# Which engine subtracts the rests of the split mixer weights: VectorE and GpSimd, or VectorE alone

## Chip, cores and metric

The kernel runs on one core of a Trainium2 chip. The metric is the time of one execution on the device in microseconds; the times given are those of several runs of the same kernel, and the profile is of one more execution.

## What is computed

Two layers of an encoder on 256 tokens of 1024 features, all in float32. Each layer is a mixer and a mixture of experts, each followed by a layernorm on 1.414 times the residual plus the result:

```python
def _hybrid_mixer(h, w_in, lb, norm_g, w_out):
    proj = jnp.einsum('bsd,dc->bsc', h, w_in)
    hq, hf_f, hf_b, hi, hg, aq, ak, av = jnp.split(proj, cuts, axis=-1)
    y_hg = _hgrn2_group(hq, hf_f, hf_b, hi, hg, lb, norm_g)
    y_att = _dilated_attention_group(aq, ak, av)
    y = jnp.concatenate([y_hg, y_att], axis=-1).astype(h.dtype)
    return jnp.einsum('bsc,cd->bsd', y, w_out)

for l in range(DEPTH):
    mix = _hybrid_mixer(h, w_in[l], lb_all[l], hg_norm_g[l], w_out[l])
    h = _layernorm(DEEPNORM_ALPHA * h + mix, ln1_g[l], ln1_b[l])
    ffn = _hier_moe(h, router_w1[l], ..., ex_w_down[l])
    h = _layernorm(DEEPNORM_ALPHA * h + ffn, ln2_g[l], ln2_b[l])
```

The eight projections of `w_in` are 512 columns each: four recurrent heads (query, two forget gates, input, output gate) and eight attention heads (query, key, value). The experts are 32, two to a token, with weights of 6.3 MB each.

## The kernel before

**Split products.** The mixer's products run on TensorE (PE in the profile) in float32r, which is faster than float32 and less exact. So each operand is split into a head, its value rounded to float32r, and a rest, what the head leaves, and a product is three: head by head, head by rest, rest by head. For the weights this happens in `split_unit` (lines 284 to 308), as the weights arrive: ScalarE (ACT) copies a quarter of a unit to float32r, the head, and a second engine subtracts the head from the weight, the rest:

```python
hd, rest_ = S.copy(wh[:, i], raw[:, i]), eng(q).tensor_sub(wl[:, i], raw[:, i], wh[:, i])
```

That is line 302. A unit is [128, 2048], a quarter [128, 512]. A projection of `w_in` has two units, so 8 quarters, and there are 8 projections in a layer; `w_out` has 4 units, 16 quarters. The first quarter of all is split in two halves. In both layers this makes 161 heads and 161 rests.

**Which engine has the rest.** `eng` is given by the caller. `chunks` (lines 310 to 316) gives VectorE (V, DVE in the profile) for the projections in `V_UNITS`, the heads' input `U_HI` and the first forget gate `U_HF`, and GpSimd (G, POOL) for the other six and, in layer 1, for `U_HI` too. `out_unit` (line 645) gives VectorE the odd quarters of `w_out` and GpSimd the even ones. GpSimd has 120 of the 161 rests, VectorE 41.

**Buffers and order.** Raw weights lie in a ring of three units, head and rest in `NB` = 4 buffers of half a slot, a quarter to each; a buffer is free once PE's products of that quarter are done, and the load of a unit waits for the split of the unit three before it. The code is written in the order in which the work depends on each other, and a scheduler makes from it one fixed list of instructions for each engine, which the engine runs in order; `tc.high_priority()` around line 302 lets a head and its rest go ahead of what else could stand there. Loads are issued from SP's list, also in order.

**The mixer in time.** The projections come in the order input `U_HI`, forget gates `U_HF` and `U_HB`, query `U_HQ`, output gate `U_HG`, then attention's `U_AQ`, `U_AK` and `U_AV`. Their products have line 321 (356 for `U_HI` in layer 1). Beside them VectorE has the recurrent heads: the gates with their cumulative sums (lines 435 to 451), the exponents of the bottom blocks (512 to 521), and five levels of block lengths 8 to 128, each with a product with the query (532), four updates of the exponents (552 to 555) and masked copies (504); PE makes the levels' scores (497, 547). L556 on GpSimd adds two score matrices. Then come the heads' outputs (576 to 590), rotary embedding (400 to 405) and splitting (413) of attention's queries and keys, the scores (613), the softmax (618 to 627), transposes (667, 668), the products with the values (673), and the output projection (642). The first layernorm, the router and the experts follow; layer 1 begins with the second layernorm's transposed and split result, and its `U_HI` weights are split while that layernorm runs.

**Experts.** For each expert 12 loads of 0.5 MB go into half slots, in a fixed rotation over 45 of them, most of which the mixer uses before; a load waits until its half slot has been read.

The functions that the change touches:

Of the kernel before, what the change touches and what calls it, by code (L numbers as in the profile page):

```python
# [20 lines left out]
P = 128  # L21
# [4 lines left out]
CAP = 32  # L26
NL = 40            # columns of the router: 4 groups, 4 of padding, 32 experts
UNIT = 2048
HALF = UNIT // 2   # what a load of expert weights fills
NSLOT = 22         # slots of 8 KB, which half a slot more follows  # L30
NB = 4             # buffers of the split weights
NR = 3             # ring of the mixer's weights
S_H = 3            # recurrent heads, 7 slots
S_Q, S_SP = 10, 11
S_KV = S_H         # keys and values, after the recurrent heads' levels
S_P2 = S_H + 1     # half of the probabilities
S_X = 15           # x transposed, in layer 0
S_XS = 16          # x split, 2 slots
S_Y = 18           # mixer's outputs split, 2 slots, half a slot to 256 of the features
S_W = 20           # split weights, half a slot to a buffer  # L40
S_T = S_H + 2      # half a slot: sums transposed
S_N = S_Q          # second layernorm's factors
# [6 lines left out]
# the order in which the loads of the experts fill what the mixer leaves behind  # L49
# [4 lines left out]
# the last round leaves alone what the next layer begins with  # L54
# [11 lines left out]
V_UNITS = (U_HI, U_HF)  # L66
# [32 lines left out]
def trunk_kernel(ctx, tc, xT, x, w_in, w_out, ex, wr, br, lbl, ng, lng, lnb, lnt, cst, msk, lmk, out,  # L99
# [20 lines left out]
    def btiles():  # L120
        """[P, 1024], a bank to each half"""
        return [psb.tile([P, 512], F32, tag="b", name=nm("b")) for _ in range(2)]

    def fresh(slot, half, dtype=F32):
        """half a slot, once its last content has been read"""
        return per.tile([P, HALF], dtype, tag=f"s{slot}_{half}", name=nm(f"s{slot}_{half}"), bufs=1)

# [12 lines left out]
    # inputs, in the order in which they are needed  # L140
# [20 lines left out]
    # sigmoid's and hidden's buffers and transposed gates; before, the router's  # L161
# [18 lines left out]
    # lb of layer 1 = softmax over the two layers, second entry  # L180
# [8 lines left out]
    class Queue:  # L189
        """an engine whose instructions keep the order of the program"""  # L190
# [9 lines left out]
    def busy(n, rhs, o=None, weights=ident):  # L200
        """products that nothing reads: an array that waits, or that works on a few columns, has its clock halved"""
        o = o or wtile()
        for _ in range(n):
            PEq.matmul(o[:, 0:rhs.shape[-1]], weights, rhs, start=True, stop=True)
# [10 lines left out]
    def deviation(c):  # L215
        """mean and 1 / deviation of the rows of chunk c"""
        Vq.bn_aggr(ln_mv[c], ln_st[c])
        Sq.activation(ln_rs[c], ln_mv[c][:, 1:2], AF.Ln, bias=epsl)
        return Sq.activation(ln_rs[c], ln_rs[c], AF.Exp, scale=-0.5)

    def shift(c):
        """-mean / deviation"""
        Vq.scalar_tensor_tensor(ln_nb[c], ln_mv[c][:, 0:1], -1.0, ln_rs[c], op0=ALU.mult, op1=ALU.mult)
# [7 lines left out]
    def normal(c, f, src, g_, b_, dst):  # L231
        """all of it without the vector engine"""
        Sq.activation(dst, src, AF.Identity, scale=ln_rs[c], bias=ln_nb[c])
        Gq.tensor_mul(dst, dst, g_[:, fs[f]])
        Gq.tensor_add(dst, dst, b_[:, fs[f]])
# [4 lines left out]
    class Areas(dict):  # L240
        """half slots of the recurrent heads"""
# [8 lines left out]
    def head_and_rest(slot):  # L250
        """h transposed, split into a float32r head and an exact float32r rest, by halves of the features"""
# [8 lines left out]
    behind = {}  # what the first heads of a layer's weights are queued behind  # L260
    for l in range(depth):
        # ------------------------------------------------------------ mixer
# [5 lines left out]
        def y_split(k, n=1):  # L268
            """head and rest of the mixer's outputs k to k + n - 1"""
# [14 lines left out]
        def split_unit(w, eng, own=None, aft=(None,) * 4, chain=False):  # L284
            """the quarters of a unit, each as head and rest, in the rotating buffers or in slots of their own"""
            for q in range(4):
# [11 lines left out]
                # the first one of all in halves  # L298
                z = (slice(0, 256), slice(256, 512)) if l == 0 and q == 0 and w is first[0] else (slice(0, 512),)
                with tc.high_priority(), after(aft[q]), after(behind.get("wh")), after(behind.get("wl")):  # L300
                    for i in z:
                        hd, rest_ = S.copy(wh[:, i], raw[:, i]), eng(q).tensor_sub(wl[:, i], raw[:, i], wh[:, i])  # L302
# [7 lines left out]
        def chunks(u, i, own=None):  # L310
            """the quarters over k of a unit of w_in, split: [P, 2, 256] head and rest"""
# [3 lines left out]
            for q, wh, wl in split_unit(w, lambda q: G if first_ or u not in V_UNITS else V, own, aft, first_):  # L315
# [7 lines left out]
        def proj_ch(u):  # L323
            """for each head % 2 [P, head // 2, t]"""
# [52 lines left out]
        # q, k, v of the attention heads  # L377
# [10 lines left out]
        def attn_in(which, ps):  # L388
            """queries or keys, transposed and split"""
# [93 lines left out]
        # [s, head, s chunk, t], t in the same chunk (A) or in the other one (Ao)  # L483
# [6 lines left out]
        def half_products(Kt, Qt, other):  # L490
            """for each head and chunk, the keys of its halves (rows) with the queries of the same or the other half"""
# [15 lines left out]
        # bottom blocks of 8: exponents relative to the middle of the block  # L507
        X = (hga["Xf"], hga["Xb"])
        for d in range(2):
# [8 lines left out]
            # reverse exponents of the keys at block length 8  # L518
# [39 lines left out]
        # silu(hg) * norm_g  # L558
# [10 lines left out]
        # o of the recurrent heads  # L569
# [25 lines left out]
        # attention: probabilities of head n, later their transposes  # L595
# [38 lines left out]
        # output projection, what it needs of the recurrent heads first  # L634
# [10 lines left out]
        def out_unit(i):  # L645
            for q, wh, wl in split_unit(mix_unit(w_out[l, i]), lambda q: V if q % 2 else G):
# [32 lines left out]
        # the first layernorm's factors: those of the second half of the features last longer  # L679
# [8 lines left out]
        # ------------------------------------------------------------ first layernorm and router  # L688
        # logits = (x W' - mean sum(W')) / deviation + b W + bias, W' = g W
# [93 lines left out]
        def choose(c):  # L783
            """the group (first of the largest) and the two experts of the tokens of chunk c"""
# [12 lines left out]
        def rank(c):  # L797
            """an expert's assignments so far, less 1000 where this is one"""
            Vq.tensor_copy(rkm[:, c], prk[c][:, 0:NE])

        def gates(c):
            """weights exp(l - first) / (1 + exp(second - first)) times the group's probability"""
# [44 lines left out]
        # the first batch's features, each in a bank of its own, so that the first tokens go ahead; the second half of  # L847
        # them gets its factors on the way to xs
# [7 lines left out]
        # ------------------------------------------------------------ experts  # L856
# [25 lines left out]
        def unit(e, i, eng=nc.sync):  # L882
            """unit i of the weights of expert e: 8 of gate and up, 4 of down"""
# [10 lines left out]
        def factors():  # L894
            """second layernorm's factors to all partitions"""
# [29 lines left out]
        def batch(b4):  # L925
# [28 lines left out]
            for e4_ in range(4):  # L954
# [12 lines left out]
                if e == 5:  # L967
                    # the queue of loads runs empty at the overflow's branch: another one has the last loads before it
# [27 lines left out]
        # windows past the first that the fullest expert needs  # L996
# [12 lines left out]
        def overflow():  # L1009
            """windows of CAP assignments past the first, where an expert has more than CAP"""  # L1010
# [163 lines left out]
```

## Time and profile before

| | |
|---|---|
| median of 3 runs | 1318.52 us (1314.72 to 1319.24) |
| profiled execution, span from first to last instruction | 1321.9 us |
| PE busy | 1008.4 us (76%) |
| DVE busy | 526.1 us (40%) |
| ACT busy | 326.2 us (25%) |
| POOL busy | 242.8 us (18%) |
| DMA | 452.83 MB, mean 343 GB/s |
| L302 on POOL, 120 instructions | 202.5 us, mean 1704 ns |
| L302 on DVE, 39 of 128x512 | 26.4 us, mean 689 ns |

Of the profiled execution the profile has the span alone, with no other time beside it; it is 3.4 us, 0.26%, above the median of the runs, which have no profile. PE is TensorE's matmuls, DVE is VectorE, ACT is ScalarE, POOL is GpSimd, SP is the engine that issues the loads. The shares are means over the whole span; the mixers take about 27 to 215 us and 652 to 875 us of it, and the rest belongs to the experts. The line of a group is a line of the kernel, and that of a helper where one records for many callers (196). A busy time counts from an instruction's start to its end and includes what it stood still in between.

### The profile page before, as it was taken

Reading aid. Unit: us, or ns where it says so; the run is one execution under the profiler, and the core shown is the slowest. Engines: PE = TensorE matmul, PEld = TensorE weight load, DVE = VectorE, ACT = ScalarE, POOL = GpSimd, SP = SyncE. Lnnn points to the kernel's source line nnn. Section 1 sums busy time; section 2 is a strip of 40 time slices with the busy share of each in tenths; the row PEclk is TensorE's granted clock in tenths of the full one; section 3 lists DMA queues with packets and bytes.
Section 4 is the critical chain, followed back from the end, with each engine's and each line's share of the span. In section 5 each row is a group of like instructions: output and inputs, shape, how many; then the busy total and the mean of one; then the engine's idle time right before and its main releaser. Section 6 shows DMA issues by size and latency. Waiting matters only on the chain.

```text
span 1321.9 us, 23713 instructions
## 1 busy us (share of the span) xinstructions
PE 1008.4 (76%) x9584; PEld 624.7 (47%) x9584; DVE 526.1 (40%) x1063; ACT 326.2 (25%) x721; POOL 242.8 (18%) x164
## 2 busy tenths in 40 slices
PE   9877998867866576767896779978777676766686
PEld 8767874434433232322496767734344242322332
DVE  4899854222222121212449997532222221212123
ACT  5546641111111010101255565311111110101011
POOL 2985431000000000000357753310000000000000
PEclk9999997888888797877898999989888887978778
DMA  7565698999999999999885356889999999999994
GB/s 275 203 242 197 219 316 289 409 396 410 413 411 410 414 409 414 410 413 413 331 285 182 107 198 228 283 333 410 378 410 411 413 409 414 409 414 412 411 413 192
DMA packets 126965, 452.83 MB, mean 343 GB/s; under 512 B 14848, under 2 KB 15744, under 8 KB 126720
## 3 DMA queue, kind: packets, MB, share of 16 engines
q1 hardware_dynamic: 125856, 448.07, 87.7%
q0 software_dynamic: 992, 3.16, 0.6%
q8 instruction: 78, 1.28, 0.4%
q14 instruction: 39, 0.32, 0.1%
HBM read 450.13 MB, written 1.05 MB: 341 GB/s over the span
## 4 chain that ended last, share of the span: by engine, by line
DMA 35%; PE 26%; DVE 13%; issue 2%; ACT 2%; DVEq 0%; SPq 0%; ACTq 0%
DMA s<-in_ex_dram 35%; PE w L870 7%; PE w L985 6%; PE w L196 3%; PE b L994 2%; DVE misc L864 2%; PE b L321 2%; PE b L642 1%; PE w L902 1%; PE w L875 1%; DVE h L196 1%; PE b L356 1%; PE b L196 1%; DVE s L532 1%; DVE misc L865 1%
## 5 line engine op out<-in xcount | busy, mean ns | idle before, releaser
L870 PE MATMUL w<-s,gbuf 128*32 128x256 f32 x3968 | 280.8, 416 | 58.6 <-DMA s<-in_ex_dram 58.3
L302 POOL TENSOR_TENSOR s<-s,s 128x512 fp32r<-128x512 f32 x120 | 202.5, 1704 | 171.0 <-ACT s L302 167.3
L870 PEld LDWEIGHTS w<-s,gbuf 128*32 128x32 f32 x3968 | 124.7, 120 | 204.7 <-DMA s<-in_ex_dram 116.1
L321 PE MATMUL b<-s,s 128*128 128x256 f32 x1440 | 196.9, 296 | 23.1 <-POOL s L302 17.6
L985 PE MATMUL w<-s,misc 128*32 128x256 f32 x2048 | 190.8, 535 | 23.2 <-ACT misc L877 22.3
L321 PEld LDWEIGHTS b<-s,s 128*128 128x128 f32 x1440 | 185.3, 200 | 30.7 <-POOL s L302 23.3
L988 DVE COPY gbuf<-w 32x256 f32<-32x256 f32 x128 | 54.1, 423 | 243.1 <-PE w L985 240.4
L875 PE MATMUL w<-cs,misc 128*128 128x128 f32 x64 | 23.6, 369 | 150.5 <-DVE misc L866 148.2
L985 PEld LDWEIGHTS w<-s,misc 128*32 128x32 f32 x2048 | 77.5, 143 | 112.6 <-issue 55.7
L863 DVE TENSOR_SCALAR misc<-misc 128x128 f32<-128x128 f32 x64 | 16.1, 252 | 278.2 <-ACT misc L862 278.2
L196 POOL DMA_DIRECT2D s<-in_lng_dram x2 | 1.0, 499 | 623.7 <-DMA s<-in_ex_dram 623.7
L302 ACT CAST s<-s 128x512 fp32r<-128x512 f32 (+1 forms) x161 | 96.8, 611 | 52.6 <-PE b L321 26.5
L875 PEld LDWEIGHTS w<-cs,misc 128*128 128x128 f32 x64 | 9.8, 153 | 184.0 <-DVE misc L866 135.8
L988 ACT COPY gbuf<-w 32x256 f32<-32x256 f32 x128 | 46.4, 363 | 198.4 <-PE w L985 197.4
L862 ACT ACTIVATE misc<-w 128x128 f32<-128x128 f32 x64 | 17.8, 278 | 268.3 <-PE w L870 264.4
L994 PE MATMUL b<-gbuf,misc 128*128 128x512 f32 x128 | 69.2, 691 | 7.9 <-DVE gbuf L988 7.9
L196 PEld LDWEIGHTS w<-oh,h 128*128 128x128 f32 x488 | 60.1, 198 | 15.6 <-issue 13.0
L196 PE MATMUL w<-oh,h 128*128 128x128 f32 x488 | 63.0, 284 | 3.3 <-issue 2.4
L864 DVE RECIPROCAL misc<-misc 128x128 f32<-128x128 f32 x64 | 61.0, 953 | 2.2
L877 ACT COPY misc<-w 128x128 f32<-128x128 f32 x64 | 17.0, 266 | 161.9 <-PE w L875 161.9
L642 PE MATMUL b<-s,s 128*128 128x512 f32 x192 | 50.5, 403 | 0.3
L934 DVE COPY gbuf<-w 128x512 f32<-128x512 f32 x14 | 9.7, 692 | 101.5 <-PE w L196 101.5
(214 smaller groups left out, 969.7 us busy)
## 6 DMA issues: line engine op xcount, KB each, us to landing
s<-in_ex_dram SPq DMA_DIRECT2D x762, 512.0 KB, 10.1
s<-in_w_in_dram SPq DMA_DIRECT2D x62, 512.0 KB, 4.3
s<-in_w_out_dram SPq DMA_DIRECT2D x16, 512.0 KB, 5.0
s<-in_ex_dram POOLq DMA_DIRECT2D x6, 512.0 KB, 6.4
s<-in_xT_dram SPq DMA_DIRECT2D x4, 256.0 KB, 5.2
h<-in_x_dram SPq DMA_DIRECT2D x1, 1024.0 KB, 6.2
gbuf<-in_lng_dram SPq DMA_DIRECT2D x4, 256.0 KB, 4.5
gbuf<-in_lnb_dram SPq DMA_DIRECT2D x4, 256.0 KB, 4.4
```

The lines of the kernel that those rows point to most:

```text
L196: return lambda *a, **k: in_order(getattr(self.eng, name)(*a, **k))
L302: hd, rest_ = S.copy(wh[:, i], raw[:, i]), eng(q).tensor_sub(wl[:, i], raw[:, i], wh[:, i])
L321: PE.matmul(o, a_, b_, start=(q == 0 and i == 0), stop=(q == 3 and i == n - 1))
L642: PE.matmul(mix[c][f], a_[:, ts_], b_, start=(k == 0 and i == 0), stop=(k == KD - 1 and i == 2))
L862: act(e_, pgu[:, 0:P], AF.Exp, scale=-1.0)
L864: V.reciprocal(e_, e_)
L870: return eng.matmul(pgu[32 * j:32 * j + 32, 0:2 * P], xsk, rhs, start=(k == 0), stop=(k == KD - 1))
L875: PE.transpose(pht[:, 0:P], hd, ident)
L877: S.copy(hdT, pht[:, 0:P])
L985: PE.matmul(pdn[q % 2][32 * q:32 * q + 32, 0:256], hdT[:, 32 * j:32 * j + 32], w[:, q * 256:(q + 1) * 256], start=(j == 0), stop=(j == 3))
L988: (V.tensor_copy if q % 2 else S.copy)(dn[32 * e4_:32 * e4_ + 32, q * 256:(q + 1) * 256], pdn[q % 2][32 * q:32 * q + 32, 0:256])
L994: PE.matmul(y[c][f], gT[:, c * P:(c + 1) * P], dn[:, fs[f]], start=False, stop=(b4 == 7))
```

## The change

All rests of line 302 are subtracted by VectorE. `split_unit` has no argument for the engine any more, `V_UNITS` is gone, and comments are left out. Nothing else in the code differs; one line less stands above, so that line 302 is line 301 after the change, 435 is 434, and so on.

```diff
-V_UNITS = (U_HI, U_HF)
...
-        def split_unit(w, eng, own=None, aft=(None,) * 4, chain=False):
+        def split_unit(w, own=None, aft=(None,) * 4, chain=False):
...
-                        hd, rest_ = S.copy(wh[:, i], raw[:, i]), eng(q).tensor_sub(wl[:, i], raw[:, i], wh[:, i])
+                        hd, rest_ = S.copy(wh[:, i], raw[:, i]), V.tensor_sub(wl[:, i], raw[:, i], wh[:, i])
...
-            for q, wh, wl in split_unit(w, lambda q: G if first_ or u not in V_UNITS else V, own, aft, first_):
+            for q, wh, wl in split_unit(w, own, aft, first_):
...
-            for q, wh, wl in split_unit(mix_unit(w_out[l, i]), lambda q: V if q % 2 else G):
+            for q, wh, wl in split_unit(mix_unit(w_out[l, i])):
```

The scheduler makes its lists anew, and they change in more than line 302. Three places follow. In the rows a name as `s_0_50_403` is a tile in half 0 of some slot, with running numbers behind; `b` and `w` are banks of PSUM, what stands before `<-` is written.

On DVE in layer 0, from the first instruction of the first forget gate on (line 435, 434 after). Before:

```order
L435 SCALAR_TENSOR_TENSOR s_1_51_404<-s_0_49_402,s_0_50_403 128x1024
L436 SCALAR_TENSOR_TENSOR s_0_49_402<-s_0_49_402,s_0_50_403 128x1024
L438 TENSOR_SCALAR s_1_51_404<-s_1_51_404 128x1024
L448 SCALAR_TENSOR_TENSOR s_0_50_403<-s_1_23_132,s_1_51_404 128x1024
L512 TENSOR_TENSOR s_0_100_841<-s_0_50_403 128x1024
L513 TENSOR_TENSOR s_0_102_843<-s_0_49_402,s_0_100_841 128x1024
L519 TENSOR_TENSOR s_0_49_402<-s_0_49_402,s_0_50_403 128x1024
L521 TENSOR_TENSOR s_0_49_402<-s_0_49_402,s_0_50_403 128x1024
```

After:

```order
L301 TENSOR_TENSOR s_1_63_499<-s_0_60_480,s_1_63_499 128x512
L434 SCALAR_TENSOR_TENSOR s_1_51_404<-s_0_49_402,s_0_50_403 128x1024
L301 TENSOR_TENSOR s_0_64_514<-s_1_61_481,s_0_64_514 128x512
L301 TENSOR_TENSOR s_1_65_529<-s_1_61_481,s_1_65_529 128x512
L435 SCALAR_TENSOR_TENSOR s_0_49_402<-s_0_49_402,s_0_50_403 128x1024
L301 TENSOR_TENSOR s_0_72_577<-s_0_70_573,s_0_72_577 128x512
L437 TENSOR_SCALAR s_1_51_404<-s_1_51_404 128x1024
L301 TENSOR_TENSOR s_1_73_592<-s_0_70_573,s_1_73_592 128x512
L447 SCALAR_TENSOR_TENSOR s_0_50_403<-s_1_23_132,s_1_51_404 128x1024
L301 TENSOR_TENSOR s_0_74_607<-s_1_71_574,s_0_74_607 128x512
L511 TENSOR_TENSOR s_0_100_841<-s_0_50_403 128x1024
L301 TENSOR_TENSOR s_1_75_622<-s_1_71_574,s_1_75_622 128x512
```

The rests of the following projections, which stood on POOL, stand between the steps of the gate, one or two to a step. From here to the first instruction of the heads' outputs on DVE (line 586) there are 46 such rows in either layer, the last four of them rests of `w_out`.

On PE in layer 0, the last products of attention's values `U_AV` (line 321, 320 after; `s_1_180_1635` is their last quarter) and what follows them. Before:

```order
L321 MATMUL b_1521<-s_1_180_1635,s_1_19_120 128x256
L321 MATMUL b_1521<-s_1_180_1635,s_1_21_122 128x256
L321 MATMUL b_1521<-s_1_180_1635,s_1_19_120 128x256 x2
L642 MATMUL b_1653<-s_0_188_1661,s_0_113_1051 128x512 x3
L642 MATMUL b_1655<-s_0_188_1661,s_0_113_1051 128x512 x3
L642 MATMUL b_1654<-s_1_189_1670,s_0_113_1051 128x512 x3
```

After:

```order
L320 MATMUL b_1521<-s_1_180_1635,s_1_19_120 128x256
L320 MATMUL b_1521<-s_1_180_1635,s_1_21_122 128x256
L320 MATMUL b_1521<-s_1_180_1635,s_1_19_120 128x256 x2
L546 MATMUL w_1013<-s_0_100_841,s_0_102_843 128x128 x4
L546 MATMUL w_1019<-s_0_100_841,s_0_102_843 128x128 x4
L575 MATMUL w_1035<-s_0_97_836,s_0_34_267 128x128
L576 MATMUL w_1035<-s_1_98_837,s_0_34_267 128x128
L575 MATMUL w_1035<-s_0_97_836,s_0_34_267 128x128
```

Before, these products stood behind the scores of attention and directly ahead of the output projection (642). Now they stand ahead of the scores of the last level (547, now 546) and of the heads' outputs (576, now 575), and so do all others of `U_AK` and `U_AV`. In layer 1 it is the same.

On DVE at the end of layer 0, where the second layernorm of the first 128 tokens begins. Before:

```order
L196 BN_STATS lnst_8_109<-b_2005 128x6
L196 BN_STATS lnst_8_109<-b_2006 128x6
L196 BN_AGGR lnmv_10_111<-lnst_8_109 128x2
L196 SCALAR_TENSOR_TENSOR h<-b_2005,lnmv_10_111,s_0_771_5102 128x512
L196 SCALAR_TENSOR_TENSOR h<-h,lnrs_12_113,s_1_772_5103 128x512
L196 SCALAR_TENSOR_TENSOR h<-b_2006,lnmv_10_111,s_0_771_5102 128x512
L196 SCALAR_TENSOR_TENSOR h<-h,lnrs_12_113,s_1_772_5103 128x512
```

After:

```order
L195 BN_STATS lnst_8_109<-b_2005 128x6
L301 TENSOR_TENSOR s_0_829_5374<-s_0_827_5370,s_0_829_5374 128x512
L301 TENSOR_TENSOR s_1_830_5377<-s_0_827_5370,s_1_830_5377 128x512
L195 BN_STATS lnst_8_109<-b_2006 128x6
L195 BN_AGGR lnmv_10_111<-lnst_8_109 128x2
L195 SCALAR_TENSOR_TENSOR h<-b_2005,lnmv_10_111,s_0_771_5102 128x512
L195 SCALAR_TENSOR_TENSOR h<-h,lnrs_12_113,s_1_772_5103 128x512
L301 TENSOR_TENSOR s_0_831_5380<-s_1_828_5371,s_0_831_5380 128x512
L301 TENSOR_TENSOR s_1_832_5383<-s_1_828_5371,s_1_832_5383 128x512
L195 SCALAR_TENSOR_TENSOR h<-b_2006,lnmv_10_111,s_0_771_5102 128x512
L195 SCALAR_TENSOR_TENSOR h<-h,lnrs_12_113,s_1_772_5103 128x512
```

Four rests of layer 1's first unit stand between the layernorm's instructions; four more stand behind the statistics of the second 128 tokens, ahead of the row that combines them (BN_AGGR).

On SP in layer 0, the six loads of the first three units of `w_out` now follow each other; before, ten loads of experts stood between the first and the sixth of them, and these now come behind. No product, head or load is added or left out.

## Rows read from the trace of the kernel before

**Rows 1.** the page, 40 slices of 33 us: busy tenths of DVE and POOL, GB/s of DMA.

```profile
DVE  4899854222222121212449997532222221212123
...
POOL 2985431000000000000357753310000000000000
...
GB/s 275 203 242 197 219 316 289 409 396 410 413 411 410 414 409 414 410 413 413 331 285 182 107 198 228 283 333 410 378 410 411 413 409 414 409 414 412 411 413 192
```

**Rows 2.** busy time by engine in three stretches (start:end, length, us and instructions), clock, DMA.

```profile
38.60:127.00 88.40, 65.85 (x623) 60.09 (x622) 86.53 (x70) 48.06 (x78) 71.42 (x37) 0.98 0.61 210
127.00:185.00 58.00, 55.63 (x347) 44.07 (x345) 36.24 (x105) 33.00 (x77) 19.39 (x15) 0.97 0.76 262
...
689.00:782.00 93.00, 68.78 (x632) 64.68 (x631) 90.31 (x80) 51.77 (x82) 68.49 (x37) 0.93 0.45 154
```

**Rows 3.** line L302: durations (min/median/max, ns) on POOL and DVE; then its share of one stretch.

```profile
L302 POOL TENSOR_TENSOR s<-s,s x120: 1272/1442/3273, 28.4 to 840.0; 128x512 fp32r<-128x512 f32 x120
...
L302 DVE TENSOR_TENSOR s<-s,s x41: 418/692/693, 5.2 to 841.3; 128x512 fp32r<-128x512 f32 x39, 128x256 fp32r<-128x256 f32 x2
...
38.60:127.00 88.40, 0.00 (x0) 20.72 (x35) 69.17 (x36) 0.98 0.61 210
```

**Rows 4.** timeline of DVE, then of POOL, layer 0: start us, us, engine, line, shapes [wait].

```profile
95.85 0.68 DVE L553 TENSOR_TENSOR s<-s,s 128x512 f32<-128x512 f32 x1
...
104.61 1.78 DVE L553 TENSOR_TENSOR s<-s,s 128x512 f32<-128x512 f32 x1
...
110.02 2.29 DVE L532 TENSOR_TENSOR s<-s,s 128x1024 f32<-128x1024 f32 x1
...
116.98 1.21 DVE L532 TENSOR_TENSOR s<-s,s 128x1024 f32<-128x1024 f32 x1
...
123.03 0.21 DVE L404 TENSOR_TENSOR s<-s,misc 128x64 f32<-128x64 f32 x1
...
123.35 1.32 DVE L401 TENSOR_TENSOR misc<-s,cs 128x64 f32<-128x64 f32 x1
...
109.81 1.42 POOL L302 TENSOR_TENSOR s<-s,s 128x512 fp32r<-128x512 f32 x1 [0.26 <-ACT s L302]
```

**Rows 5.** groups of DVE by line and form: count | busy us, mean ns | idle before.

```profile
L532 DVE TENSOR_TENSOR s<-s,s 128x1024 f32<-128x1024 f32 x10 | 15.9, 1587 | 0.1
...
L553 DVE TENSOR_TENSOR s<-s,s 128x512 f32<-128x512 f32 x8 | 12.0, 1503 | 0.0
...
L516 DVE TENSOR_TENSOR s<-s,s 128x1024 f32<-128x1024 f32 x4 | 9.2, 2304 | 0.0
...
L552 DVE TENSOR_TENSOR s<-s,s 128x512 f32<-128x512 f32 x8 | 9.2, 1149 | 0.1
...
L512 DVE TENSOR_TENSOR s<-s 128x1024 f32<-128x1024 f32 x4 | 8.6, 2162 | 0.2
...
L401 DVE TENSOR_TENSOR misc<-s,cs 128x64 f32<-128x64 f32 x8 | 8.3, 1032 | 0.2 <-issue 0.2
```

**Rows 6.** L321 in one stretch (PE busy and count first); timelines of PE and DVE, layer 0.

```profile
127.00:185.00 58.00, 17.45 (x125) 16.18 (x125) 0.97 0.76 262
...
147.81 8.54 PE L321 MATMUL b<-s,s 128*128 128x256 f32 x69
...
156.19 6.63 PE L642 MATMUL b<-s,s 128*128 128x512 f32 x24
...
142.86 0.42 DVE L618 CUSTOM_DVE_ANT_0 s<-w,gbuf 128x256 f32<-128x256 f32 x1 [1.56 <-PE w L613]
...
160.89 1.28 DVE L302 TENSOR_TENSOR s<-s,s 128x512 fp32r<-128x512 f32 x2
```

**Rows 7.** timeline of POOL between the layers: start us, us.

```profile
652.51 2.54 POOL L302 TENSOR_TENSOR s<-s,s 128x512 fp32r<-128x512 f32 x2 [7.61 <-ACT s L302]
...
659.85 5.98 POOL L302 TENSOR_TENSOR s<-s,s 128x512 fp32r<-128x512 f32 x4 [0.78 <-ACT s L302]
```

**Rows 8.** line L302 on DVE: what its idle time before ended on (us, times).

```profile
  ACT s L302: 27.3, 26
```

## The prediction

> **What bounds the kernel now.** I read the slices of the page first [rows 1]. Two stretches of each layer differ: in the expert stages the loads move some 410 GB/s, in the two mixers (slices 0 to 6 and 20 to 27) 107 to 333 while DVE rises to 9, and POOL is busy only there. The expert weights are a fixed number of bytes, and the loads run into half slots that the mixer leaves free, so I take a microsecond off a mixer as a microsecond off the end: the loads behind it start sooner and are the same loads.
>
> The table by stage [rows 2] cuts each mixer in two. In the first part (38.6 to 127 us, 689 to 782 us: gates and the five levels of the recurrent heads) DVE is busy 86.5 of 88.4 us and 90.3 of 93 us. PE has 22 us of gaps there. In the second part (127 to 185: attention and most of the output projection; layer 1 repeats it) PE is busy 55.6 of 58 us and DVE 36.2. So DVE sets the first part and PE the second.
>
> Next the split line L302 [rows 3]: 120 rests on POOL, median 1.44 us, and 41 on DVE, median 0.69. In the first part of layer 0 POOL runs 36 of them for 69 us, so each is far above the 1.27 us of the shortest. What stretches them, stretches DVE too [rows 4]: L553 takes 1.78 us at one place and 0.68 at another, L532 takes 2.29 us beside a POOL rest that starts 0.2 us before it, and 1.21 us where none does, and of two instructions of 64 columns L401 takes 1.32 us and L404 0.21. The excess is the same whatever the length: 1.10, 1.08 and 1.11 us. I read it as DVE standing still for one POOL rest, and POOL for one DVE instruction.
>
> **The change part by part.** It takes 120 rests from POOL and gives them to DVE; ACT's heads, PE's products and the loads are the same in number.
>
> 1. First part of each mixer, relief. At most all 36 rests hold DVE once: 36 x 1.09 = 39 us. From below, the forms of [rows 5] against their undisturbed lengths: six lines of 1024 columns, four each, 2.16 to 2.30 us, 24 x (2.22 - 1.21) = 24; L532 10 x 0.38 = 4; L553 8 x 0.82 = 7; L552 8 x 0.47 = 4; L401 8 x 0.82 = 7. Together 46 us in two layers, 23 a layer, with a dozen smaller groups not counted. I take 33, between the ends, since the timeline shows most rests hitting something.
>
> 2. The same part, added work. By the order, 46 rests now stand on DVE between the first L435 and the first L586 of a layer (42 of w_in and 4 of w_out). Two in a row take 1.28 us [rows 6], so 0.64 each: 29 us. Net of 1 and 2: -4 us a layer, bounds -10 and +6.
>
> A rule that speaks against the change: the Trainium skill, Perfetto Trace Analysis, section Optimizing Scalar/DVE Operations, says that work may be moved off a saturated DVE, to ScalarE or even to GPSIMD. By that alone the change would cost 29 us a layer. The same section warns that the two share a read port, so that moving between them might not help, and there [rows 4] agrees. SBUF — State Buffer, section Who interferes with whom, says that a DVE instruction with two SBUF inputs and a GpSimd one that reads SBUF exclude each other for a whole instruction; at the shortest rest, 1.27 us, relief would be up to 46 us, where the rows show 1.09 each.
>
> 3. Waits in that part. A rest waits for ACT's head, which waits for a split buffer that PE must have read four quarters ago. A quarter is 12 products at 0.124 us (69 in 8.54 [rows 6]), 1.5 us, against (87 - 33 + 29) / 46 = 1.8 us of DVE work to a rest. With what comes to it under 4, PE's count is closer still: 65.9 + 15 = 81 us of the 84 that are left. PE keeps ahead by a little; I add 1.5 us a layer, bounds 0 and 5.
>
> 4. Second part. By the order, PE now does all products of the keys and values (U_AK, U_AV) before the last level, where it had gaps; before, 125 of them ran in the second part [rows 6]. That is 125 x 0.124 = 15 us out of a stretch in which PE was busy 55.6 of 58. Left for PE are 41 us; DVE has 36 there, less some 2 for six rests that no longer hold it, plus 4 more of its own, 3. The softmax, which began at 142.9, waited for the keys; its products, ACT's exponentials and DVE follow each other and do not shrink with PE. Gain between 0 (the chain of attention sets the end) and 15 (PE sets it); I take 8, near the middle. The remaining rests of the output projection, 12 on DVE for 8 on POOL and 8 on DVE, lie beside the products of that projection, 24 in 6.63 us [rows 6], with PE never idle there; without that cover they would cost 4 x 0.64 = 2.6 us.
>
> 5. From layer 0 to layer 1. Eight rests of the first unit stand on DVE between the layernorm's instructions; on POOL they took 2.54 us for two and 5.98 for four [rows 7]. At most 8 x 0.64 = 5 us are added to the chain statistics, centring, transposes; but the first tokens' products (48) need no second chunk and keep PE going. I add 1.5 us, bounds 0 and 5.
>
> 6. Free: POOL's queue empties, and what stays on it (L556, the layernorm's factors, three loads at expert 5) starts no later. On SP, six loads of w_out now stand together ahead of some ten expert loads that stood between them. Ten are 5.2 MB, 13 us at 410 GB/s; the share of 0.76 in the second part [rows 2] leaves 58 x 0.24 = 14 us, and w_out's loads go earlier, since the rests that free their ring do. Nothing, then, or up to 4 us a layer if that room is not there.
>
> Sum: 2 x (-4 + 1.5 - 8) + 1.5 = -19.5 us. The profiled execution has a span of 1321.9 us, 3.4 above the median of the runs, so the span goes to about 1302 and the runs to **1299 us**, faster by 1.5%. What a measurement of this kernel can tell from no change is about 0.5%, 6.6 us.
>
> **The rivals.**
> - *The attention does not follow* (term 4 near 1 us, the rest as above): 2 x (-4 + 1.5 - 1) + 1.5 = -5.5, **1313 us**. For it: DVE's first attention instruction waits for PE [rows 6], and DVE, ACT and PE take turns. Against: what it waited for were the keys, whose last products ran in that part.
> - *DVE waits in order* (slower). DVE runs its list in order; with rests ahead of the levels' steps, each wait for a head stops the recurrent chain too. DVE waited 27.3 us before 26 of its 41 rests [rows 8], 1.05 us each, where PE set the pace. In the first parts are 92 rests; from 19.5 / 92 = 0.21 us each the gain is gone. At 0.45 us each, 41 us: -19.5 + 41 = +22, **1340 us**. Against: the 1.8 us of DVE work to a rest, longer than PE's quarter.
> - *No relief* (the stretched DVE instructions have another cause): 2 x (29 - 8) = +42, **1360 us**. [Rows 4] speak against it, almost alone. It is also what the sentence of Perfetto Trace Analysis in the Trainium skill, cited under 2, would lead one to.
> - *The loads take it back*: the SP order or the slots hold the expert stage, -19.5 + 2 x 4 or more, 1307 to 1318 us.
>
> **How the numbers follow.** Forecast 0.64, its own range 1283 to 1312 (terms 1 to 5 about half way to their bounds); attention 0.16; waits in order 0.11; no relief 0.03; loads 0.06. Faster by over 0.5% (under 1312): the forecast but 0.01, a quarter of the attention rival, 0.04, half of the loads, 0.03: 0.70. Within: 0.01 + 0.12 + 0.03 = 0.16. Slower: 0.11 + 0.03 = 0.14. The range leaves out the far ends of terms 1 and 4 (relief of 38 and all 15 us, twice, would be near 1275) and most of the waits: 1276 to 1322, with some 0.04 below and 0.13 above.
>
> **What would show it.** Right: POOL without L302; L553 at 0.68 and L512 at about 1.2 us throughout; DVE still near 97% in the first part, which ends 2 to 5 us sooner; L613 closer behind L586, and the last L668 some 8 us sooner against it. Wrong: idle time of DVE before L302 put down to ACT above 0.2 us a rest in the first part, lengths that stay at 2.2 us without POOL, or an expert stage whose DMA share falls under that of now.

## The result, and the profile after

The changed kernel takes **1282.66 us** (median of 4 runs, 1281.85 to 1286.23) where the kernel before takes 1318.78 beside it: a ratio of 0.974 with a 95% interval of 0.972 to 0.976. That is 36 us less, inside the range on record (1276 to 1322), a third of a microsecond under the range of the forecast itself (1283 to 1312), and nearly twice its 19.5 us. The profiled execution's span went from 1321.9 to 1284.4 us.

The page of the changed kernel: span, busy time of each engine, then two lines of the 40 slices of 32 us. Its line numbers are one below those of the kernel before (L301 was L302).

```profile
span 1284.4 us, 23653 instructions
...
PE 1002.8 (78%) x9584; PEld 623.8 (49%) x9584; DVE 519.1 (40%) x1183; ACT 326.7 (25%) x721; POOL 42.4 (3%) x44
...
DVE  5998753222222121212369988642222221212124
POOL 1001011000000000000100000200000000000000
```

POOL is nearly empty in both mixers (a 2 at most), where [rows 1] have up to 9 in layer 0 and 7 in layer 1. DVE has 120 instructions more than before and is busy for less: 519.1 us, where the page before has 526.1.

The same cut by stage as in [rows 2], for both layers (start:end, length; busy us and instructions of PE, PEld, DVE, ACT, POOL; clock; DMA share; GB/s). The cuts are the first L434 of a layer, its first L585, and L697.

```profile
36.80:122.90 86.10, 78.43 (x758) 76.26 (x756) 83.20 (x126) 57.44 (x94) 3.83 (x1) 0.96 0.79 269
122.90:165.80 42.90, 41.90 (x220) 30.18 (x221) 31.34 (x99) 24.55 (x62) 0.00 (x0) 0.92 0.70 240
676.60:768.40 91.80, 79.58 (x759) 77.30 (x757) 87.12 (x142) 60.39 (x98) 2.83 (x1) 0.93 0.58 194
768.40:808.40 40.00, 39.00 (x221) 27.87 (x222) 31.04 (x97) 24.45 (x62) 0.00 (x0) 1.00 0.70 244
```

Of the kernel before, the second part of layer 1, which [rows 2] did not show:

```profile
782.50:840.40 57.90, 55.56 (x345) 43.86 (x344) 36.44 (x106) 33.02 (x77) 19.22 (x15) 0.97 0.74 261
```

So the first parts are still DVE's, nearly full, now with 126 and 142 instructions on it; PE's gaps in them have shrunk from 22 to 8 us in layer 0. The second parts have 125 and 124 products less, and PE is still busy in all but 1 us of each. The whole account, in us, from the starts of the instructions named (the last L993 by its end, and the starts are those of each timeline):

| stretch | before | after | change | forecast |
|---|---|---|---|---|
| start to the first L434 | 38.6 | 36.8 | -1.8 | 0 |
| first part, layer 0 (to L585) | 88.3 | 86.0 | -2.3 | -2.5 |
| second part, layer 0 (to L697) | 58.0 | 42.9 | -15.1 | -8 |
| router and experts, layer 0 (to the last L993) | 470.5 | 473.7 | +3.2 | 0 |
| from there to the first L434 of layer 1 | 33.5 | 37.2 | +3.7 | +1.5 |
| first part, layer 1 | 93.6 | 91.7 | -1.9 | -2.5 |
| second part, layer 1 | 58.0 | 40.0 | -18.0 | -8 |
| router and experts, layer 1 | 472.1 | 466.6 | -5.5 | 0 |
| the rest | 9.4 | 9.4 | 0 | 0 |

Two rows carry it: the second parts, 33 of the 37.5 us. What made the start 1.8 us shorter was not looked into.

Groups of DVE by form, answering [rows 5] and the DVE line of [rows 3] (count | busy us, mean ns | idle before); the rests in the first part of each layer, DVE's before ScalarE's heads; and what DVE's idle time before the rests ended on (us, times), answering [rows 8]:

```profile
L301 DVE TENSOR_TENSOR s<-s,s 128x512 fp32r<-128x512 f32 x159 | 109.5, 701 | 34.5 <-ACT s L301 32.8 <-DMA s<-in_w_in_dram 1.2
...
L531 DVE TENSOR_TENSOR s<-s,s 128x1024 f32<-128x1024 f32 x10 | 14.3, 1428 | 0.0
...
L552 DVE TENSOR_TENSOR s<-s,s 128x512 f32<-128x512 f32 x8 | 5.5, 686 | 0.0
...
L511 DVE TENSOR_TENSOR s<-s 128x1024 f32<-128x1024 f32 x4 | 4.9, 1218 | 0.0
L515 DVE TENSOR_TENSOR s<-s,s 128x1024 f32<-128x1024 f32 x4 | 4.9, 1218 | 0.0
L400 DVE TENSOR_TENSOR misc<-s,cs 128x64 f32<-128x64 f32 x8 | 1.7, 210 | 0.0
...
36.80:122.90 86.10, 33.08 (x46) 28.02 (x46) 0.96 0.79 269
676.60:768.40 91.80, 30.91 (x46) 27.48 (x46) 0.93 0.58 194
...
  ACT s L301: 32.8, 40
```

L515 went from 2304 to 1218 ns, L511 from 2162 to 1218, L552 from 1503 to 686 and L400 from 1032 to 210. The same instructions, with nothing on POOL beside them, take half as long or a fifth. L531's mean of 1428 ns hides the same: nine of its ten take 1.21 to 1.23 us, and one, in layer 1 beside the addition L555 that is left on POOL, 3.31. The waits for ScalarE's heads grew from 27.3 to 32.8 us in the whole kernel, but they lie where PE sets the pace; in layer 1's first part there is one, of 1.5 us.

### The profile page after: what moved, and what is told of

Same layout as the page of the kernel before. It is cut to its first block, busy times and chain, and to the rows that moved or that the text cites. A ratio compares the mean times of both kernels' runs of the same rounds, so it can differ in the third digit from the quotient of the medians.

```text
span 1284.4 us, 23653 instructions
## 1 busy us (share of the span) xinstructions
PE 1002.8 (78%) x9584; PEld 623.8 (49%) x9584; DVE 519.1 (40%) x1183; ACT 326.7 (25%) x721; POOL 42.4 (3%) x44
## 5 line engine op out<-in xcount | busy, mean ns | idle before, releaser
L984 PE MATMUL w<-s,misc 128*32 128x256 f32 x2048 | 195.2, 545 | 22.9 <-ACT misc L876 22.0
L320 PE MATMUL b<-s,s 128*128 128x256 f32 x1440 | 177.7, 285 | 2.7 <-ACT s L301 2.6
L320 PEld LDWEIGHTS b<-s,s 128*128 128x128 f32 x1440 | 174.4, 192 | 4.6 <-ACT s L301 3.4
L301 DVE TENSOR_TENSOR s<-s,s 128x512 fp32r<-128x512 f32 (+1 forms) x161 | 110.3, 697 | 34.5 <-ACT s L301 32.8
L301 ACT CAST s<-s 128x512 fp32r<-128x512 f32 (+1 forms) x161 | 97.1, 613 | 54.4 <-PE b L320 31.0
L993 PE MATMUL b<-gbuf,misc 128*128 128x512 f32 x128 | 71.2, 708 | 7.9 <-DVE gbuf L987 7.9
L641 PE MATMUL b<-s,s 128*128 128x512 f32 x192 | 53.9, 419 | 0.0
L993 PEld LDWEIGHTS b<-gbuf,misc 128*128 128x128 f32 x128 | 27.9, 230 | 48.8 <-issue 30.7
```

Of the source, the lines that this page charges most:

```text
L301: hd, rest_ = S.copy(wh[:, i], raw[:, i]), V.tensor_sub(wl[:, i], raw[:, i], wh[:, i])
L320: PE.matmul(o, a_, b_, start=(q == 0 and i == 0), stop=(q == 3 and i == n - 1))
L641: PE.matmul(mix[c][f], a_[:, ts_], b_, start=(k == 0 and i == 0), stop=(k == KD - 1 and i == 2))
L984: PE.matmul(pdn[q % 2][32 * q:32 * q + 32, 0:256], hdT[:, 32 * j:32 * j + 32], w[:, q * 256:(q + 1) * 256], start=(j == 0), stop=(j == 3))
L993: PE.matmul(y[c][f], gT[:, c * P:(c + 1) * P], dn[:, fs[f]], start=False, stop=(b4 == 7))
```

## The experiments

All times below stand beside runs of the kernel before on the same chip. The stage lengths are cut at the same instructions as in the table above (an added line shifts the line numbers by one or two), and come from the one profiled execution of each kernel.

### 1. The output projection's rests back on GpSimd

The parameter eng of the split is back, with VectorE for all units of the input projections, and for the output projection what the kernel before has:

```diff
-            for q, wh, wl in split_unit(mix_unit(w_out[l, i])):
+            for q, wh, wl in split_unit(mix_unit(w_out[l, i]), lambda q: V if q % 2 else G):
```

> Every second rest of the output projection's weights goes back to GpSimd, 16 in all; the rests of the input projections stay on VectorE. Theory A (the second part got shorter because 124 products of the projections left it): nothing depends on these rests, since TensorE is busy 42.1 of 43.1 us there; 1280 to 1287 us, second part 41 to 45 us. Theory B (the second part got shorter because the output projection's own rests no longer take GpSimd's 1.3 to 3.3 us): a good part of the 15 and 18 us comes back, 1295 to 1310 us.

1287.15 us (1279.87 to 1291.59, 5 runs), ratio 0.977 [0.975, 0.980], which just overlaps that of the change; the median lies 0.15 us above theory A's range, and the profile is of the fastest of the five. The second parts are 42.6 and 39.7 us long, as after, with six of the rests on POOL in each. Theory A: what shortened the second parts is not in these rests. Whether they cost the few microseconds by which the median is higher is not shown.

### 2. The same order, with GpSimd's work put back beside it

Three kernels in which VectorE, TensorE and ScalarE have the instructions of the changed kernel in its order, and GpSimd gets one more behind each of 96 rests. None of its outputs is read. The edit of the first; dup is true for the six units that the expectation names:

```diff
                         hd, rest_ = S.copy(wh[:, i], raw[:, i]), V.tensor_sub(wl[:, i], raw[:, i], wh[:, i])
+                        if dup:
+                            G.tensor_sub(raw[:, i], raw[:, i], wh[:, i])
```

**The subtraction** (two operands read):

> As after, with the same order of instructions on VectorE, TensorE and ScalarE, but GpSimd repeats 96 of the rests (units HB, HQ, HG, AQ, AK, AV) behind VectorE's own, into the raw weights, and no one reads what it writes. TensorE waits for none of them. Theory A (a subtraction on GpSimd lengthens what VectorE does beside it, by 1.09 us each): some 40 of them fall into each first part, so +44 us of VectorE there, less some 3 us of slack; first part 120 to 130 us, 1350 to 1375 us in all. Theory B (the collisions were incidental, and the kernel before lost its time in TensorE's 23 us of waits for GpSimd's slower rests): VectorE's rows keep the lengths of after, 1278 to 1290 us.

1367.35 us (1364.22 to 1375.34), ratio 1.039 [1.035, 1.044]: 85 us slower than the change. Both parts of layer 0 and the first of layer 1 in the table by stage, the added line's durations on POOL (min/median/max, ns), two waits in the first part of layer 0 (us, times, longest), and a piece of the timeline:

```profile
38.50:165.70 127.20, 85.21 (x742) 79.80 (x740) 124.07 (x126) 57.22 (x93) 86.87 (x44) 0.92 0.55 186
165.70:205.80 40.10, 39.04 (x221) 27.90 (x222) 31.36 (x99) 24.46 (x63) 0.00 (x0) 1.00 0.75 255
711.20:845.10 133.90, 90.67 (x758) 84.28 (x756) 130.01 (x142) 60.49 (x97) 83.79 (x45) 0.90 0.41 134
...
L303 POOL TENSOR_TENSOR s<-s,s x96: 1267/1682/3182, 28.6 to 822.1; 128x512 f32<-128x512 f32 x96
...
ACT s L301 <- POOL s L303: 23.7, 15, 3.2
...
DVE s L301 <- ACT s L301: 0.7, 1, 0.7
...
105.58 1.21 DVE L522 TENSOR_TENSOR s<-s,s 128x1024 f32<-128x1024 f32 x1
105.74 2.21 POOL L303 TENSOR_TENSOR s<-s,s 128x512 f32<-128x512 f32 x1 [0.63 <-DVE s L301]
106.72 1.78 DVE L301 TENSOR_TENSOR s<-s,s 128x512 fp32r<-128x512 f32 x1
```

The same 126 instructions of DVE fill 124.1 us instead of 83.2. The timeline shows how: L303 starts while L522 runs and takes 2.21 us, 0.94 more than the shortest, about as long as L522 still runs (to 106.79); the next instruction of DVE then takes 1.78 instead of the 0.69 of a rest alone. The first part grew from 86.0 to 127.2 us with 43 subtractions in it, 0.96 us each; in layer 1 from 91.7 to 133.9 with 44, again 0.96 (a mean over all of them, whatever each met), and above the 120 to 130 expected. No product waits for these subtractions. ScalarE does: they read the head, and a later head goes into its buffer. But VectorE waited only once for a head, for 0.7 us, and is idle for 3.1 us of the part, where it is for 2.9 in the changed kernel: what grew is its own busy time. So theory B is out. The second parts, with the projections' products gone and nothing of the kind on POOL, are 40 us long here too.

**The memset** (nothing read), with this line in its place:

```diff
+                            G.memset(raw[:, i], 0.0)
```

> The same as the run with the repeated subtractions, at the same places, but GpSimd writes a constant into the raw weights (a memset, which reads nothing). If any instruction of GpSimd holds VectorE up, each costs about its own length of some 0.6 us: +24 us in each first part, 1320 to 1335 us. If it takes an instruction that reads two operands on both engines: nothing, 1279 to 1290 us.

1285.10 us (1277.15 to 1286.68), ratio 0.974 [0.970, 0.978]: as the change.

```profile
37.80:123.90 86.10, 78.44 (x757) 76.27 (x755) 83.19 (x126) 57.43 (x93) 27.25 (x44) 0.96 0.78 269
...
L303 POOL MEMSET s<- x96: 525/527/1013, 29.7 to 747.1; 128x512 f32 x96
...
105.62 1.22 DVE L533 TENSOR_TENSOR s<-s,s 128x1024 f32<-128x1024 f32 x1
105.81 0.53 POOL L303 MEMSET s<- 128x512 f32 x1 [1.33 <-issue]
```

POOL is busy 27 us of the first part and DVE has the 83.2 us that it has without; the memset runs in its 0.53 us in the middle of L533, which keeps its 1.22. POOL being busy costs nothing by itself.

**The copy** (one operand read):

```diff
+                            G.tensor_copy(raw[:, i], wh[:, i].bitcast(F32))
```

> As the runs with repeated subtractions and with memsets, but GpSimd copies the head into the raw weights: one operand is read. If what counts is that GpSimd reads: each of the some 38 in a first part costs VectorE its length, first part 100 to 118 us, 1325 to 1367 us. If it takes two operands on GpSimd as well: first part 81 to 84 us, 1279 to 1290 us.

1309.11 us (1304.05 to 1314.40), ratio 0.994 [0.991, 0.997], between the two cases, so that both missed it; the first parts, 101.4 and 106.1 us, lie low in the first case's 100 to 118.

```profile
37.50:138.90 101.40, 81.51 (x757) 77.38 (x755) 98.22 (x126) 57.22 (x93) 57.60 (x44) 0.97 0.67 228
...
L303 POOL COPY s<-s x96: 611/1017/2552, 29.4 to 766.5; 128x512 f32<-128x512 f32 x96
```

43 copies made the first part 15.4 us longer, 0.36 us each. So it takes an instruction that reads, and a copy costs DVE a bit under 40% of a subtraction; the price lies below the copy's shortest length of 0.61 us as the subtraction's lies below its 1.27. I had expected the whole length. Whether the second operand or the greater length makes the subtraction dearer is not separated here.

The Trainium skill, SBUF — State Buffer, section Who interferes with whom, says that a VectorE instruction with two SBUF inputs contends with a GpSimd one that reads SBUF and not with one that only writes, and that the shared ports are an exclusive lock, which whoever issues first has for the whole instruction. The first agrees with these three runs (0.96, 0.36 and 0 us an instruction); of the second, 43 x 1.27 = 55 us would be an estimate, where the trace shows 41.

### 3. The values' products behind the scores again

```diff
+        late = None
...
-            aft = [behind.get((i, q)) if u == U_HI else None for q in range(4)]
+            aft = [behind.get((i, q)) if u == U_HI else late if u == U_AV else None for q in range(4)]
...
-            V.reciprocal(den[:, n], den[:, n])
+            late = V.reciprocal(den[:, n], den[:, n])
```

> As after, but the heads and rests of unit AV wait for the last reciprocal of the attention's probabilities, so that 88 of the 96 products of AV stand behind the scores again (69 in the kernel before, none in after). Theory A (order: the second part is as long as TensorE's products in it): second part +88 x 0.124 = +11 us, first part shorter by at most 8 rests of 0.65 us, so +5 to +11 us a layer: 1293 to 1305 us. Theory B (the second part got shorter because VectorE's rows in it are not held up by GpSimd any more): 1279 to 1288 us.

1308.56 us (1307.61 to 1310.10), ratio 0.994 [0.992, 0.996]: 26 us slower than the change, 4 more than the upper end of theory A. Both parts of layer 0, and the projections' products within the second:

```profile
36.20:114.20 78.00, 68.58 (x669) 66.47 (x667) 76.25 (x115) 51.63 (x83) 4.14 (x1) 0.93 0.73 246
114.20:175.90 61.70, 52.54 (x308) 41.91 (x309) 39.40 (x109) 31.09 (x73) 0.00 (x0) 0.89 0.72 241
...
114.20:175.90 61.70, 12.75 (x88) 12.52 (x88) 0.89 0.72 241
```

With POOL as empty as after, the second part goes from 42.9 to 61.7 us (layer 1: 40.0 to 62.3) and the first from 86.0 to 78.0 (91.7 to 81.1). The 88 products brought 12.75 us of PE's time back; PE also idles 9 us there, which it does not after, half of it in one wait:

```profile
137.24 12.75 PE L322 MATMUL b<-s,s 128*128 128x256 f32 x88 [4.69 <-DVE s L301]
```

The edit holds back the heads and rests of the values too, until the last reciprocal (136.44 us), and PE, in its order, waits for the first of these rests. So the 18.8 us are not the place of the products alone: 12.75 are, the idle time grew by 8, and the other products took 2 less. Net, a layer is 10.8 and 11.7 us longer. That is about 60% of what both parts of a layer gained together (17.4 and 19.9 us). So the relief on VectorE alone doesn't shorten the second part, and the products that stand in it do lengthen it, by what PE needs for them at least.

### 4. The second layer's first eight rests back on GpSimd

Here too with the parameter eng:

```diff
-            for q, wh, wl in split_unit(w, own, aft, first_):
+            for q, wh, wl in split_unit(w, lambda q: G if first_ else V, own, aft, first_):
```

First the changed kernel again, beside the next two kernels and the copies above:

> The changed kernel itself, timed again beside the next three: 1282 to 1286 us, and as the measure of what the expert stages do by themselves from one execution to the next (they differed by up to 6 us between the profiles so far).

1283.24 us (1276.48 to 1288.26, 6 runs), ratio 0.973 [0.970, 0.977]. Its stage lengths repeat those of the first profile within 1 us, also the experts' 473.6 and 467.5.

> As after, but the first eight rests of the second layer's mixer go back to GpSimd. Theory A (they cost at the boundary of the layers, because they stand between the steps of the layernorm on VectorE that the mixer's inputs wait for): from the last product of the first layer's experts to the scan 43 to 44 us instead of 45.9, 1279 to 1282 us. Theory B (the boundary's 2 us come from loads or from noise): 45 to 46 us there, 1282 to 1286 us.

1277.63 us (1274.97 to 1284.44, 6 runs), ratio 0.971 [0.968, 0.975]. Times and the stage below lie a little under theory A's ranges. By the times alone it can't be told from the change; by the stages it can. From the last L993 to the first L434 it is 33.5 us, exactly what the kernel before has, where after has 37.2 (to the scan, the measure of the expectation: 42.2 against 45.9). In the changed kernel DVE does this there:

```profile
636.95 0.70 DVE L195 BATCH_NORM_STATS2 lnst<-b 128x6 f32<-128x512 f32 x1 [0.82 <-PE b L993]
637.56 1.27 DVE L301 TENSOR_TENSOR s<-s,s 128x512 fp32r<-128x512 f32 x2
638.76 0.69 DVE L195 BATCH_NORM_STATS2 lnst<-b 128x6 f32<-128x512 f32 x1
...
639.73 0.75 DVE L195 SCALAR_TENSOR_TENSOR h<-b,lnmv,s 128x512 f32<-128x512 f32 x1
640.58 0.75 DVE L195 SCALAR_TENSOR_TENSOR h<-h,lnrs,s 128x512 f32<-128x512 f32 x1
641.25 1.28 DVE L301 TENSOR_TENSOR s<-s,s 128x512 fp32r<-128x512 f32 x2
```

Two pairs of rests, 2.55 us, stand inside the layernorm's chain, and the mixer's first products wait for its end. Theory A. The profiled executions differ by more than that, and not all of it is the edit's: 3 us lie in the second part of layer 0, ahead of it (last section).

### 5. The last reader on GpSimd

In the changed kernel one instruction of GpSimd is left in each first part, A + A2 (L555). The next kernel keeps the edit of experiment 4, moves that addition to VectorE and sixteen small operations of the second layer from VectorE to ScalarE; the last one moves the addition alone.

```diff
-        G.tensor_add(A, A, A2)
+        V.tensor_add(A, A, A2)
```

And in the first of the two:

```diff
-                    V.tensor_scalar(g[:, sl], g[:, sl], oml[:, i:i + 1], lb1[:, i:i + 1],
-                                    op0=ALU.mult, op1=ALU.add)
-                    V.tensor_scalar_sub(a[:, sl], a[:, sl], lno[:, i:i + 1])
+                    act(g[:, sl], g[:, sl], AF.Identity, scale=oml[:, i:i + 1], bias=lb1[:, i:i + 1])
+                    act(a[:, sl], a[:, sl], AF.Identity, bias=lno[:, i:i + 1])
...
+            V.tensor_scalar_mul(lno, lno, -1.0)
```

> As the run before, and VectorE also takes GpSimd's last addition of the mixer (A + A2, 3.3 us there, during which a rest on VectorE took 2.9 us), while 16 small operations of the second layer (g times a factor plus a bound, a minus a factor) go from VectorE to ScalarE. If the first part is still bound by VectorE (78 of 81 and 83 us): 1 us less in the first layer, 4 to 6 less in the second, 1273 to 1279 us. If TensorE (73 and 71 us) or the chain through ScalarE already sets it: 1279 to 1285 us.

1272.10 us (1265.84 to 1275.06, 6 runs), ratio 0.966 [0.962, 0.969]; first parts 83.0 and 88.2 us. The median is 0.9 us under the lower of the two ranges.

> As the run with the first eight rests on GpSimd and A + A2 on VectorE, without the 16 operations on ScalarE. If the addition alone gave what that combined run gained in its first parts (3.2 us in the first layer, 1.3 in the second): first parts 83 and 86 to 88 us, 1268 to 1273 us in all. If the operations on ScalarE gave a part: second layer's first part 89 to 90 us, 1273 to 1277 us.

**1269.58 us** (1262.10 to 1272.15, 6 runs), ratio 0.964 [0.961, 0.967]; first parts 83.3 and 88.1 us. The addition did all that can be seen, and the 4 to 6 us expected in layer 1 from the sixteen operations did not come. The first part of layer 1, with the operations moved and then without:

```profile
660.20:748.40 88.20, 78.30 (x757) 76.29 (x756) 81.94 (x127) 66.73 (x113) 0.00 (x0) 0.94 0.65 214
...
661.70:749.80 88.10, 78.01 (x758) 75.79 (x756) 86.21 (x143) 60.37 (x97) 0.00 (x0) 0.96 0.66 215
```

VectorE did get 4.3 us less to do, and ScalarE 6.4 more; VectorE is idle for 6.3 us instead of 1.9, 3.5 of them in six waits for ScalarE's heads, of which there are none without the operations. So VectorE no longer sets that part by itself. The last version beats both kernels, by 46 and, by the ratios beside the kernel before, 13 us. Why one addition is worth 3 us in layer 0: first the run of experiment 4, where it is still on POOL, the last steps of the first part,

```profile
108.53 3.83 POOL L555 TENSOR_TENSOR s<-s,s 128x1024 f32<-128x1024 f32 x1 [104.49 <-ACT s L540]
...
110.04 3.47 DVE L301 TENSOR_TENSOR s<-s,s 128x512 fp32r<-128x512 f32 x2
...
114.79 3.76 PE L546 MATMUL w<-s,s 128*128 128x128 f32 x16 [3.95 <-DVE s L531]
```

then the last kernel:

```profile
110.30 1.21 DVE L555 TENSOR_TENSOR s<-s,s 128x1024 f32<-128x1024 f32 x1
...
111.43 1.34 DVE L301 TENSOR_TENSOR s<-s,s 128x512 fp32r<-128x512 f32 x2
...
114.05 2.02 PE L546 MATMUL w<-s,s 128*128 128x128 f32 x16 [1.81 <-DVE s L531]
```

On POOL it took 3.83 us and held a pair of rests for 2.1 us more than they need; on DVE it takes 1.21. (It has the place of another instruction of 1.21 us, L562, which the scheduler put behind L531.) PE then waits 1.81 us for L531 instead of 3.95, and the 16 products behind that wait take 2.02 us instead of 3.76: the clock is higher there (last section).

## Why the prediction was right, and where its size was off

**Relief (1) and added work (2): right, each a little low.** DVE's 83.2 us of layer 0's first part hold 46 rests of 33.1 us and so 50.1 us of other work, where [rows 2] have 86.5 without any rest: 36 us less, and some 34 in layer 1, for the 33 taken. The rests cost 33.1 and 30.9 us for the 29 taken: most stand alone, at 0.69 us and not at 0.64 as in a pair, and one of layer 0 takes 2.87 beside L555. The two misses offset each other. Net -2.3 and -1.9 us with the waits, -2.5 forecast. The price of a collision was 1.09 us by three rows of the timeline; experiment 2 gives 0.96 over 43.

**Waits (3): right.** DVE idles 2.9 us in that part where it idled 1.9, none of it before a rest (none above 0.2 us), and PE keeps ahead with 78.4 us busy. In layer 1 one rest waited 1.5 us.

**Second part (4): this is the step that was mis-sized.** The text took 8 us out of 0 to 15, "near the middle", because the softmax's products, ScalarE's exponentials and VectorE "follow each other and do not shrink with PE". It measured 15.1 and 18.0. PE was busy 55.6 of 57.9 us before and 39.0 of 40.0 after in layer 1: as soon as the products were gone, the chain of attention fitted into what PE still had to do, and PE set the end of the part as before. The removed products cost 55.56 - 39.00 = 16.6 us by PE's busy time, 0.13 each, and the gaps shrank by another 1.4; at the 0.124 us of the prediction they were 15. The chain had begun early enough too: the first scores stand 8.6 us behind the first L585 instead of 14.5. A stretch that is 96% one engine should have been given to that engine, and 15 taken. With it the sum would have been -33.5 us, and 1285. In experiment 3, 88 of the products are back, and the part is longer by their time and more.

**Boundary (5): under-sized, within its bounds.** 3.7 us for the 1.5 taken (0 to 5). The step let the first tokens' products cover the rests; by the timeline of experiment 4 two pairs already stand ahead of what those products wait for. Without the eight rests on DVE all of it comes back.

**Free (6): not shown to be nothing.** The expert stages came out 3.2 us longer and 5.5 shorter. Over all eleven profiles of this study they are 466.4 to 473.7 us long, with the same instructions of TensorE. No run singles out why, and it stays open; the two come to -2.3 us together.

**The rivals.** *The attention does not follow* (1313) fell with term 4. *DVE waits in order* (1340) fell with that one wait of 1.5 us in both first parts. *No relief* (1360) is close to what experiment 2 made with its subtractions, 1367, but that the two numbers are near is in part luck: against the kernel before the first parts grew by 39 and 40 us, where the rival adds 29, and the second parts shrank by 18 each, where it takes 8. The experiment also shows that the new order, with the collisions left in, is a loss: the second parts' whole gain is there, and the first parts pay more than twice as much for it.

The signs named beforehand came out: POOL without the split's rests, L552 at 0.69 and L511 at 1.22 us, DVE at 97% of the first part (95% in layer 1), the scores closer behind L585. The last copy of attention's transposed probabilities (L667) came 12 us sooner against L585, and 15 in layer 1, not 8, which is term 4 again.

## What to carry to other kernels

When two engines work beside each other, compare one instruction with itself: the same shape at 0.68 and 1.78 us in one timeline can be the price of the other engine, and work that such an engine does "for free" may cost the bounding one more than doing it itself would. After such a move, ask what the engines with gaps can now do earlier; the larger part of the gain came from products that filled PE's gaps in one stretch and left another, which PE bounded. And leave alone the few moves that land inside a dependent chain, as those of the layernorm here.

## What the runs showed of the hardware

Beside a VectorE that was 97% busy, a memset on GpSimd cost it nothing, a copy 0.36 us and a subtraction 0.96; a predicated copy on VectorE, which reads PSUM and a mask, kept its mean of 742 to 743 ns in all three.

The clock accounts for 2.9 us of layer 0's second part. That part is 42.9 us long at a mean granted clock of 0.92 in the changed kernel, and 40.0 at 1.00 in layer 1 and in experiment 4, with the same products. TensorE alone in layer 0, by stretches (length, busy us and products, clock, DMA share, GB/s), first the changed kernel:

```profile
115.00:120.00 5.00, 4.36 (x19) 0.50 0.71 257
...
135.00:140.00 5.00, 4.75 (x26) 0.80 0.38 120
140.00:145.00 5.00, 5.00 (x16) 0.52 0.69 243
```

then experiment 4:

```profile
115.00:120.00 5.00, 4.75 (x21) 0.50 0.66 232
...
135.00:140.00 5.00, 4.98 (x31) 1.00 0.40 114
140.00:145.00 5.00, 5.00 (x25) 1.00 0.81 270
```

and the last kernel:

```profile
115.00:120.00 5.00, 3.18 (x27) 1.00 0.96 341
...
140.00:145.00 5.00, 5.00 (x27) 1.00 0.96 372
```

In the first two the clock is at the lower of its two levels, 1.2 GHz, from 115 to 120 us, right after the 4 us for which PE waits before L546; in the last kernel, where that wait is 1.8 us, it is at 2.4 GHz. A wait of that length doesn't decide it: the other kernel of experiment 5 has the same 1.81 us, and its 16 products take 3.42. In the changed kernel it falls a second time, between 135 and 145 us, with means of 0.80 and 0.52; in the other two it stays at 2.4 GHz there. Up to the end of that part experiment 4 has the same instructions on TensorE, VectorE and ScalarE in the same order as the changed kernel, so their order alone doesn't decide it. No run looked for the cause of that second fall.
